# A two-layer diffusion backbone on one core: Pool's queue put in order by hand, modulation tiles requested one ahead, the last FFN product ended by output tile, and context squares moved

## The chip, the cores and the metric

The kernel runs on one core of one Trainium2 chip, as a single program. The metric is the device time of one execution in microseconds (us). The time before is a median of 1727.9 us over 3 runs (1726.85 to 1728.54).

A core has a matrix engine (TensorE, PE in the profile; PEld is its weight load), a vector engine (VectorE, DVE), an activation engine (ScalarE, ACT), GpSimd (POOL) and SyncE (SP). Here SP and POOL mainly issue DMA transfers; POOL's are those that add into their target, the saves of intermediate results, and most modulation tiles.

## The reference

Two transformer layers over 512 latent tokens with a context of 256 tokens, width 1024. Both token streams share the weights.

```python
for i in range(DEPTH):                      # DEPTH = 2
    mx = split(silu(c) @ ada_w[i] + ada_b[i], 6)        # shift, scale, gate; twice
    mc = split(silu(c_ctx) @ ada_w[i] + ada_b[i], 6)
    h_x = rms_norm(x, g1) * (1 + mx[1]) + mx[0]
    h_c = rms_norm(y_ctx, g1) * (1 + mc[1]) + mc[0]
    # layer 0: windowed attention with a sink; layer 1: retention in both directions
    out_c, out_x = mixer[i](h_x, h_c)
    x = x + mx[2] * out_x
    x = x + mx[5] * swiglu(rms_norm(x, g2) * (1 + mx[4]) + mx[3], ffn_w_in[i], ffn_w_out[i])
    if i == 0:                              # the context stream, likewise, with mc
        ...
return x
```

Layer 1 needs the context only as input of its keys and values. The modulation vectors of layer 1 (`mx`, `mc` of i = 1) are matrix-vector products of 1024 by 6144.

## The kernel before

Tokens lie along the free axis, features along the 128 partitions, so a [1024, 512] activation is eight tiles of 128 x 512. Each float32 operand is split into a high part (a cast to fp32r by ScalarE, `whi`) and a low part (the difference, by VectorE, `wlo`); a product is three matmuls: high by high, low by high, high by low (`split`, L169 and L170).

The stage that the diff touches is the FFN of layer 0 and the passage into layer 1. The FFN runs on latent and context tokens together (768 columns, two halves of 384, `THIRDS`), and both its products use a scheme of seven block products of half size.

**Loop over hidden tiles.** `pos` runs from 2 to 21. `seven(pos, jobs)` issues seven products of 12 matmuls; between them VectorE and ScalarE split the weights of this position and the next, and finish the activation of the position before (`last_gate`). After each odd position `pair_sums` (in the next position) forms sums and saves four tensors to device memory, four DMAs from POOL (L1063, L1065). `jobs[0]` follows the third product and `jobs[2]` the last: from position 5 both are `ada_next`, which computes one column of layer 1's modulation: a tile of 128 x 1024 weights is loaded by POOL into the tile `adaw` (one buffer) and VectorE multiplies it with the broadcast condition row and sums along it (L278), once or, for the tiles of both streams, twice.

At the ends of some positions stand steps that prepare weight sums for the second product in device memory: copies from SP and accumulating DMAs from POOL (`sum_add`, L824, 1280 KB each). Those within this loop stand at the ends of positions 3, 5, 7, 9, 11, 13 and 15; the accumulating ones are at 5, 7, 11 and 15.

**Second product.** For each of seven products (`prod`) there are 11 pairs of hidden tiles, two to a step (`m` from 0 to 5, the last step one pair). `fo_step` runs a step: for each pair, for each of four output tiles `d`, three matmuls. `fo_add` adds finished sums, scaled by the gate, to the streams: `xr` (latent) and `cres` (context). In the first five products every even step also does an `ada_next`; in the last product `late_sums` squares the new residual (`add_squares`), sums squares over the partitions by matmuls with a matrix of ones (`context_squares` for the context, `first_rms` for the first half of the latents), and normalises (`latent_norm`).

**Into layer 1.** `fo_add(o, 0, 1)` adds the last four output tiles. `values_first` runs the first product of the values (24 matmuls of 512 columns), then the last four context squares and their sums, the context norm (`context_norm`), the second half's row sum (`rms`) and its normalisation follow; then values, keys and queries.

**Order.** A planner lays out each engine's instructions from its own estimate of when each becomes ready. In the stretch `with tc.manual_schedule(engines=Hand)`, which covers the loop and the second product, the named engines take the program's order instead; instructions from outside the stretch may still be placed between. Before, `Hand` names PE, DVE, Activation and SP, so POOL's DMAs are the planner's. `after(ins, others)` adds an order without a semaphore. A buffer that is asked for again is waited for until its last reader is done, wherever the request stands in the program.

Of the kernel before, what the change touches and what calls it, by code (L numbers as in the profile page):

```python
# [11 lines left out]
AF = mybir.ActivationFunctionType  # L12
# [42 lines left out]
def dit_kernel(ctx, tc, xT, cT, crow, small, consts, masks, tabs0, tabs1, jtab, adaQ, adaN, adaT, wst, wgu, wfo, out):  # L55
# [37 lines left out]
    order = mybir.DependencyInfo(mybir.DependencyClass.NoSync, mybir.DependencyReason.DATA)  # L93
    turn = {"pre": None, "lnexp": [], "silu": []}

    def after(ins, others):
# [93 lines left out]
    def t_sq(n):  # L190
        return T(rp, 512, "sq", 2)[:, :n]
# [76 lines left out]
            silu(cr[:, i * 1024:(i + 1) * 1024], cr[:, i * 1024:(i + 1) * 1024])  # L268
        return cr

    def ada_tile(l, part, d, streams, cr, behind, room):

        j = part * 8 + d
        w, res = T(room, 1024, "adaw", 1 if l else 3), []
        (nc.gpsimd if l else nc.sync).dma_start(w, adaT[l, j])
        for s in streams:
            junk = T(rp, 1024, "y0", 1, BF16) if l else T(room, 1024, "junk", 1, BF16)
            res.append(nc.vector.tensor_tensor_reduce(junk, w, cr[:, s * 1024:(s + 1) * 1024], 1.0,  # L278
                                                      sm_t[:, C_ADAB + l * 48 + j:C_ADAB + l * 48 + j + 1], mult, add,
                                                      mods[l, s][:, part, d:d + 1]))  # L280
            after(res[-1], behind)
        return res
# [829 lines left out]

    def ada_next(behind=()):

        if ada_q:
            ada_tile(*ada_q.pop(0), cr, behind, fp)

    L_, R_ = slice(0, 512), slice(512, 1024)
    tile = {}
# [115 lines left out]
        split(fo[i][1], *w)  # L1235
        fo[i][1] = w

    def fo_step(i, o, first):
        x, w = fo.pop(i)
        n = x[0].shape[1] // 384  # L1240
        m = FO[i][1]
        for j in range(n):
            xs = [t[:, j * 384:(j + 1) * 384] for t in x]
            for d in range(4):
                ws = slice(j * 512 + d * P, j * 512 + (d + 1) * P)
                for e, (p, r) in enumerate(((w[0], xs[0]), (w[1], xs[0]), (w[0], xs[1]))):
                    nc.tensor.matmul(o[d], p[:, ws], r, start=first and 2 * m + j + e == 0,  # L1247
                                     stop=2 * m + j == PAIRS - 1 and e == 2, skip_group_check=True)

    def fo_add(o, d0, half, minus=False):  # L1250
        ends = []
# [22 lines left out]
    def context_squares(ds, first, last, behind=()):  # L1274
        for d in ds:
            sq = t_sq(SC)
            nc.scalar.activation(sq, cres[d], AF.Square)
            ins = nc.tensor.matmul(ctx_sum[0], ones, sq, start=d == first, stop=d == last, skip_group_check=True)
            after(ins, behind)
        return ins  # L1280

    def unit(u):
        w = [T(hq, 768, "aq", 20)[:, 0:512] for _ in range(KT - 4 * (u == 11))]
# [7 lines left out]
    ada_both = [(1, part, d, (0, 1)) for part in (0, 1) for d in range(KT)]  # L1291
    ada_one = [(1, part, d, (0,)) for part in (2, 3, 4, 5) for d in range(KT)]
    ada_q = [t for pair in zip(ada_both, ada_one) for t in pair] + ada_one[16:]
    wsel[0] = 0
    raws = [0]
    cr = None
# [60 lines left out]
    def nothing():  # L1357
        pass
# [16 lines left out]
    with tc.manual_schedule(engines=Hand):  # L1375
        for pos in range(2, FT):
            jobs = [nothing] * 3
            if pos == 2:
                jobs = [last_sum, gates_negated, nothing]
            elif pos == 3:  # L1380
                jobs[0] = rows_begin
            elif pos == 4:
                jobs[2] = rows_silu
            else:
# [12 lines left out]
        o = fo_y  # L1397
        for i, (prod, m) in enumerate(FO):
            if m == 0 and prod:
                o = fo_y if prod in (2, 4) else fo_z if prod == 5 else [bank("X"), bank("X"), pj(384), pj(384)] \  # L1400
                    if prod in (1, 3) else [bank("Y"), bank("Z"), bank("Z"), bank("Y")]
                if prod == 3:
                    fo_z = o
            if i == 0:
                fo_split_weights(1)
                last_gate(FT - 1)
            if i + 2 < len(FO):
                fo_split_weights(i + 2)
                fo_split_tokens(i + 2)
                fo_load(i + 3)  # L1410
            fo_step(i, o, prod in (0, 1, 3, 6))
            if m == (PAIRS - 1) // 2:
                for args in (((0, 0),), ((0, 0),), ((4, 0, True),), ((4, 1),), ((4, 1, True), (0, 1)), ((4, 0),), ())[prod]:
                    fo_add(o, *args)
            if prod < 5:
                ada_next() if m % 2 == 0 else None
            elif prod == 5:
                early_sums(m)
            else:
                late_sums(m)  # L1420
            if i == 2:
                Q.close()
                H = ExitStack()
                hpool[0] = H.enter_context(tc.tile_pool(name="hR", bufs=1, reuse_waits="tile", side="right"))
                h_rest += [(T(hpool[0], 512, "aq", 11, F32R), T(hpool[0], 512, "aq", 11, F32R)) for _ in range(4)]
                h_first += [T(hpool[0], 512, "aq", 11, F32R) for _ in range(3)]
                off_grid(hpool[0], 16)
                h_first.insert(0, T(hpool[0], 512, "aq0", 1, F32R))
                hm += [T(hpool[0], 512, "qk", 8) for _ in range(KT)]
    assert not ada_q  # L1430
    fo_add(o, 0, 1)
    F.close()
    E.close()

# [81 lines left out]
                                           stop=k == 3 and i == 2, skip_group_check=True)  # L1516
        return ins

    def product_v(os, a, w, first, tiles=(0, 1), by_k=False):

        for t, k in ((t, k) for k in range(4) for t in tiles) if by_k else ((t, k) for t in tiles for k in range(4)):
            tok = slice(t * P, t * P + P)
            whi, wlo = (p[:, k % 2 * 512:k % 2 * 512 + 512] for p in w[k // 2])
            xhi, xlo = (x[:, tok] for x in a(k))
            for i, (p, r) in enumerate(((xhi, whi), (xhi, wlo), (xlo, whi))):
                ins = nc.tensor.matmul(os[t], p, r, start=first and k + i == 0, stop=k == 3 and i == 2,  # L1526
                                       skip_group_check=by_k or not first)
        return ins
# [11 lines left out]
            res.append((hi, lo))  # L1540
        return res

    def strips(hd, behind=()):

        jt = T(qp, 1152, "rj", 1)
        nc.sync.dma_start(jt, jtab)
# [4 lines left out]
        lnexp(dx[:, 0:384], jt[:, 0:384], AF.Exp, scale=nlb, bias=dcol[:, 2, hd:hd + 1])  # L1551
# [4 lines left out]
        lnexp(dcx, jt[:, 0:640], AF.Exp, scale=lf, bias=dcol[:, 0, hd:hd + 1])  # L1556
        sums = []
        for c in (slice(0, 320), slice(320, 640)):
            e = t_hn(320) if hd else pj(320)
# [16 lines left out]
    def values_first(w, by_k=False):  # L1576

        Y = [W4("Z"), W4("Z")]
        ins = product_v(Y, quarter_of("11"), w, True, by_k=by_k)
# [3 lines left out]
        return w, Y, vt, ins  # L1583

    def context_values(w):
        c = [pj(), pj()]
# [2 lines left out]

    wsel[0] = 2  # L1590
    b11 = first_weights_v(0)
    b11, Yv, vt, ins = values_first(b11, True)
    context_squares(range(4), 4, 3, [ins])
    normed = context_norm([])
    add_squares(T1, range(4))
    rms(0, HALVES[1], behind=[ins])
    latent_norm(1, range(KT))
    for hd in range(RH):
        bq = chunk_base + 16 * hd
# [18 lines left out]
        k11, k21 = split_chunk(r11), split_chunk(r21)  # L1618
        if hd == 0:
            sums = token_sums(hm, 0, T(qp, 16, "sh2", 1), h_sum, [normed], (sub, add))  # L1620
            dx, dcx = strips(0, [sums])
        cos1, sin1 = rope_tables()
        Y, X, kc = W4("Y"), W4("X"), W4("X")
        kt, qt = [[T(qa, 512, "gate", 4) for _ in range(2)] for _ in range(2)]
# [212 lines left out]
            gated(t)  # L1837
        if not last:

            b11, Yv, vt, ins = values_first(first_weights_v(hd + 1))  # L1840
            transposes(1)
            transposes(0)
            turned(slice(0, SX))
# [365 lines left out]
```

## Time and profile before

| | us |
|---|---|
| median of 3 runs (lowest, highest) | 1727.9 (1726.85, 1728.54) |
| profiled execution | 1730.67 |
| its span, first to last instruction | 1728.7 |
| TensorE busy | 1685.8 |
| VectorE busy | 1340.9 |
| ScalarE busy | 893.1 |
| POOL busy | 116.6 |

The mean granted TensorE clock is 0.992 of full speed. In the profiled execution the loop over hidden tiles lies at 403 to 714 us from the span's start, the second product at 714 to 885, the first values of layer 1 behind that.

How to read the rows. An instruction in order of time has start, duration, engine, line, operation, output<-input, shape, and, in brackets, how long its engine stood idle before it and what ended that. A row of waits has total us, times, longest. A stretch of time has its length, then the busy time of PE, PEld, DVE, ACT and POOL with instruction counts, then the granted clock, the busy share of the DMA engines and GB/s. A DMA row ends with count, size of each and us from issue to landing; where there are several, that is the median. The "chain that ended last" lists pieces with start, duration and count.

### The profile page before, as it was taken

The page shows a single profiled execution, that of the slowest core. Times are in us where ns is not written, and L with a number is a line of the kernel's source. Part 1 is how long each engine was busy: PE and PEld are TensorE (multiplying, and loading weights), DVE is VectorE, ACT ScalarE, POOL GpSimd, SP SyncE. Part 2 cuts the span into 40 slices and gives each one's busy share as a digit, 9 for nine tenths or more (in the row PEclk, how much of TensorE's full clock was granted, in tenths as well). Part 3 has the DMA queues.
Part 4 walks back from the last instruction along what each step waited for, and adds up shares of the span by engine and source line. Part 5 has one row for each costly group of instructions (what it writes and reads, how often), then busy time and mean ns, then how long its engine had stood idle before and what let it go on. Part 6 is the DMA issues. An engine that isn't in the chain of part 4 may idle for free.

```text
span 1728.7 us, 27887 instructions
## 1 busy us (share of the span) xinstructions
PE 1685.8 (98%) x10798; PEld 1526.5 (88%) x10798; DVE 1340.9 (78%) x2395; ACT 893.1 (52%) x1565; POOL 116.6 (7%) x246
## 2 busy tenths in 40 slices
PE   8999999999989899999998999999999999999999
PEld 5878877899989899999978888888898899999997
DVE  6788888797678779778779857767757898876874
ACT  5678878474434334444555534534525565444442
POOL 0011111000111112100000000000000000000000
PEclk9999999999999999999999999999999999999999
DMA  9848967644867776898662634624624323333322
GB/s 383 303 93 195 238 141 190 219 153 159 253 194 240 246 219 213 302 307 286 196 160 61 187 107 103 184 69 124 193 64 110 122 74 106 114 109 110 100 86 85
DMA packets 113316, 293.87 MB, mean 170 GB/s; under 512 B 9520, under 2 KB 20288, under 8 KB 112928
## 3 DMA queue, kind: packets, MB, share of 16 engines
q1 hardware_dynamic: 87696, 218.75, 38.4%
q0 software_dynamic: 25200, 72.82, 17.8%
q8 instruction: 84, 1.38, 0.3%
q10 hardware_dynamic: 288, 0.52, 0.1%
q14 instruction: 48, 0.39, 0.1%
HBM read 274.82 MB, written 61.28 MB: 194 GB/s over the span
## 4 chain that ended last, share of the span: by engine, by line
PE 55%; DVE 6%; DMA 4%; issue 3%; ACT 1%; POOL 0%; POOLq 0%; DVEq 0%; ACTq 0%; SPq 0%
PE Y L965 8%; PE Z L1526 7%; PE Z L965 4%; PE Y L1515 3%; DMA adaw<-in_adaT_dram 3%; PE Y L1247 2%; PE Z L1247 2%; PE pj L152 2%; PE pj L154 2%; PE pj L153 2%; PE pj L1526 2%; PE pj L1247 2%; PE X L1247 2%; PE X L965 2%; PE X L1515 1%
## 5 line engine op out<-in xcount | busy, mean ns | idle before, releaser
L169 ACT CAST whi<-wraw 128x1024 fp32r<-128x1024 f32 (+1 forms) x285 | 295.3, 1040 | 323.3 <-PE Y L965 48.8
L170 DVE TENSOR_TENSOR wlo<-wraw,whi 128x1024 fp32r<-128x1024 f32 (+1 forms) x285 | 343.7, 1209 | 119.4 <-ACT whi L169 118.4
L965 PE MATMUL Y<-aq,whi 128*128 128x384 f32 x640 | 174.4, 338 | 0.0
L965 PE MATMUL Y<-aq,wlo 128*128 128x384 f32 x320 | 109.2, 341 | 13.3 <-DVE wlo L170 13.2
L965 PEld LDWEIGHTS Y<-aq,whi 128*128 128x128 f32 x640 | 118.4, 191 | 0.2
L278 DVE CUSTOM_DVE_ANT_0 y<-adaw,crow,small_sb 128x1024 bf16<-128x1024 f32 x64 | 82.1, 1282 | 43.5 <-DMA adaw<-in_adaT_dram 42.8
L1526 PE MATMUL Z<-whi,sA 128*128 128x512 f32 x256 | 80.6, 391 | 0.0
L106 ACT ACTIVATE pr<-pr,stat,qs 128x513 f32<-128x513 f32 (+2 forms) x96 | 74.1, 774 | 11.2 <-DVE stat L728 11.1
L965 PEld LDWEIGHTS Y<-aq,wlo 128*128 128x128 f32 x320 | 61.0, 191 | 15.7 <-DVE wlo L170 15.7
L152 PE MATMUL pj<-ax,whi 128*128 128x512 f32 x176 | 69.2, 393 | 0.5 <-DVE res L261 0.5
L154 PE MATMUL pj<-ax,whi 128*128 128x512 f32 x176 | 68.7, 390 | 0.0
L153 PE MATMUL pj<-ax,wlo 128*128 128x512 f32 x176 | 68.6, 390 | 0.0
L747 PE MATMUL pT<-const_sb,pr 128*128 128x128 f32 x352 | 56.6, 286 | 2.3 <-DVE pr L738 1.1
L261 DVE SCALAR_TENSOR_TENSOR res<-pj,mod,res 128x512 f32<-128x512 f32 (+1 forms) x64 | 45.3, 713 | 16.9 <-PE pj L154 16.8
L965 PE MATMUL Y<-sA,whi 128*128 128x256 f32 x304 | 58.1, 277 | 0.0
L722 DVE CUSTOM_DVE_ANT_0 pr<-S,mask,qs 128x256 f32<-128x256 f32 (+1 forms) x96 | 53.4, 567 | 5.6 <-PE S L721 4.4
L1526 PEld LDWEIGHTS Z<-whi,sA 128*128 128x128 f32 x256 | 48.0, 188 | 10.4
L965 PE MATMUL Y<-hx,whi 128*128 128x256 f32 x304 | 56.3, 277 | 0.0
L1247 PE MATMUL Y<-aq,whi 128*128 128x384 f32 x176 | 54.2, 343 | 0.0
L1247 PE MATMUL Z<-aq,whi 128*128 128x384 f32 x176 | 52.4, 338 | 0.0
L1526 PE MATMUL Z<-wlo,sA 128*128 128x512 f32 x128 | 50.5, 394 | 1.0 <-DVE wlo L170 1.0
L747 PEld LDWEIGHTS pT<-const_sb,pr 128*128 128x128 f32 x352 | 41.4, 145 | 11.2 <-issue 4.3
(591 smaller groups left out, 5102.4 us busy)
## 6 DMA issues: line engine op xcount, KB each, us to landing
wraw<-in_wst_dram SPq DMA_DIRECT2D x158, 512.0 KB, 3.7
adaw<-in_adaT_dram POOLq DMA_DIRECT2D x48, 512.0 KB, 4.0
op<-saved SPq DMA_DIRECT2D x35, 384.0 KB, 5.8
saved<-op POOLq DMA_DIRECT2D x33, 384.0 KB, 6.8
wraw<-in_wgu_dram SPq DMA_DIRECT2D x24, 512.0 KB, 4.7
gu_sum<-in_wgu_dram SPq DMA_DIRECT2D x8, 1280.0 KB, 13.2
gu_sum<-in_wgu_dram POOLq DMA_DIRECT2D x8, 1280.0 KB, 13.2
wraw<-fo_sum SPq DMA_DIRECT2D x20, 512.0 KB, 5.2
```

The costliest lines, as they stand in the source:

```text
L106: ins = nc.scalar.activation(*args, **kw)
L152: nc.tensor.matmul(o, whi, xhi, start=first, stop=False)
L153: nc.tensor.matmul(o, wlo, xhi, start=False, stop=False)
L154: return nc.tensor.matmul(o, whi, xlo, start=False, stop=last)
L169: after(nc.scalar.copy(hi, t), behind)
L170: return nc.vector.tensor_tensor(lo, t, hi, op=sub)
L278: res.append(nc.vector.tensor_tensor_reduce(junk, w, cr[:, s * 1024:(s + 1) * 1024], 1.0, sm_t[:, C_ADAB + l * 48 + j:C_ADAB + l * 48 + j ...
L747: nc.tensor.transpose(tp[:, a * P:(a + 1) * P], self.pr[(0, 2, 1, 3)[a]][:, ki * P:(ki + 1) * P], ident)
L965: nc.tensor.matmul(o, p, r, start=first and k + i == 0, stop=k == 3 and i == 2, skip_group_check=not first)
L1247: nc.tensor.matmul(o[d], p[:, ws], r, start=first and 2 * m + j + e == 0, stop=2 * m + j == PAIRS - 1 and e == 2, skip_group_check=True)
L1515: ins = nc.tensor.matmul(o[:, e * SC:(e + 1) * SC], p[:, ws], r, start=first and k + e + i == 0, stop=k == 3 and i == 2, skip_group_check= ...
L1526: ins = nc.tensor.matmul(os[t], p, r, start=first and k + i == 0, stop=k == 3 and i == 2, skip_group_check=by_k or not first)
```

## The change

Five edits. Modulation tiles are requested by a step of their own, `ada_ahead`, right behind the use of the tile before. POOL joins the engines ordered by hand, and within that stretch `after` adds no order. In the last product the steps `m` = 4 and 5 are joined, and the matmuls of the three pairs run output tile by output tile. Context squares 4 to 7 are formed two steps to one step sooner, and only their summing matmuls stay behind; the last additions `fo_add(o, 0, 1)` and the squares of what they make (`last_squares`) move into the hand-ordered stretch. The first values of layer 1 are cut in two, with the four context sums, the context norm and the row sum of the second half between the halves, TensorE's order there by hand.

```diff
     def after(ins, others):
-        for o in others:
+        for o in others if not by_hand[0] else ():
             tc.add_manual_dep(ins.ins, o.ins.name, order, reason="table set turn")
...
+    def ada_load(l, part, d, room):
+        w = T(room, 1024, "adaw", 1 if l else 3)
+        (nc.gpsimd if l else nc.sync).dma_start(w, adaT[l, part * 8 + d])
+        return w
...
     def ada_next(behind=()):
+        args = ada_q.pop(0)
+        ada_tile(*args, cr, behind, fp, ada_w.pop())
+        ada_ahead()
+
+    def ada_ahead():
         if ada_q:
-            ada_tile(*ada_q.pop(0), cr, behind, fp)
+            ada_w.append(ada_load(*ada_q[0][:3], fp))
...
-    def fo_step(i, o, first):
+    def fo_step(i, o, first, joined=False):
...            # parts_: the pairs of step i, and of i + 1 if joined
+        if joined:
             for d in range(4):
+                for part in parts_:
+                    one(*part, d)
+        else:
+            for part in parts_:
+                for d in range(4):
+                    one(*part, d)
...
+    def context_square(d, sq):
+        nc.scalar.activation(sq, cres[d], AF.Square)
+        ctx_sq[d] = sq
...            # context_total(ds, ...): the matmuls with ones over ctx_sq[d]
     def late_sums(step):
         if step < 2:
             add_squares(T0, (4 + 2 * step, 5 + 2 * step))
+            for d in (4 + 2 * step, 5 + 2 * step):
+                context_square(d, t_hn(SC))
         if step == 1:
             ctx_sum.append(pj(SC))
-        if step in (1, 2):
-            context_squares((2 * step + 2, 2 * step + 3), 4, 3)
-        if step == 1:
+            context_total((4, 5), 4, 3)
             first_rms()
+        if step == 2:
+            context_total((6, 7), 4, 3)
...
+    def last_squares():
+        y, c = ssq[0], slice(384, SX)
+        for d in range(4):
+            t = t_hn(512) if d < 2 else t_sq(512)
+            context_square(d, t[:, 0:SC])
+            sq = t[:, SC:SC + P]
+            nc.scalar.activation(sq, xr[d][:, c], AF.Square)
+            nc.vector.tensor_tensor(y[:, c], y[:, c], sq, op=add)
...
-    Hand = {mybir.EngineType.PE, mybir.EngineType.DVE, mybir.EngineType.Activation, mybir.EngineType.SP}
+    Hand = {mybir.EngineType.PE, mybir.EngineType.DVE, mybir.EngineType.Activation, mybir.EngineType.SP,
+            mybir.EngineType.Pool}
...            # position 4: ada_ahead() for the first tile
             for st in sum_turns.get(100 + pos, ()):
-                st(end)
+                st(None)
...
+            last = prod == 6 and m == (PAIRS - 3) // 2
+            if i + 1 < len(FO) or last:
+                fo_step(i, o, prod in (0, 1, 3, 6), last)
...
+        fo_add(o, 0, 1)
+        last_squares()
+        by_hand[0] = False
     assert not ada_q
-    fo_add(o, 0, 1)
...
-    b11, Yv, vt, ins = values_first(b11, True)
-    context_squares(range(4), 4, 3, [ins])
-    normed = context_norm([])
-    add_squares(T1, range(4))
-    rms(0, HALVES[1], behind=[ins])
+    ends = []
+
+    def totals():
+        context_total(range(4), 4, 3)
+        ends.append(context_norm([]))
+        ends.append(rms(0, HALVES[1]))
+
+    with tc.manual_schedule(engines={mybir.EngineType.PE}):
+        b11, Yv, vt = values_first(b11, totals)     # totals between k = 0, 1 and k = 2, 3
+    normed, other_rms = ends
     latent_norm(1, range(KT))
```

Two exponentials in `strips` are ordered behind the row sum of the second half (`soon=[other_rms]`).

More of the change, by code (lines that the diff above doesn't have):

```diff
@@ L1236, in fo_split_weights, with one @@
         fo[i][1] = w
-    def fo_step(i, o, first):
[L1239 to L1243, printed above, removed]
-            for d in range(4):
[L1245 to L1248, printed above, removed]
+    def fo_step(i, o, first, joined=False):
+        parts_, end = [], [fo.pop(j) for j in ((i, i + 1) if joined else (i,))]
+        k = 2 * FO[i][1]
+        for x, w in end:
+            n = x[0].shape[1] // 384
+            for j in range(n):
+                parts_.append((k, [t[:, j * 384:(j + 1) * 384] for t in x], w, j * 512))
+                k += 1
+        def one(k, xs, w, c, d):
+            ws = slice(c + d * P, c + (d + 1) * P)
+            for e, (p, r) in enumerate(((w[0], xs[0]), (w[1], xs[0]), (w[0], xs[1]))):
+                nc.tensor.matmul(o[d], p[:, ws], r, start=first and k + e == 0,
+                                 stop=k == PAIRS - 1 and e == 2, skip_group_check=True)
+        if joined:
+            for d in range(4):
+                for part in parts_:
[4 more added lines that the diff above has]
+                    one(*part, d)
     def fo_add(o, d0, half, minus=False):
@@ L1272, in add_squares, with context_total @@
                 nc.vector.tensor_tensor(ssq[0][:, cols], ssq[0][:, cols], sq, op=add)
-    def context_squares(ds, first, last, behind=()):
+    def context_square(d, sq):
+        nc.scalar.activation(sq, cres[d], AF.Square)
+        ctx_sq[d] = sq
+    def context_total(ds, first, last, behind=()):
         for d in ds:
-            sq = t_sq(SC)
-            nc.scalar.activation(sq, cres[d], AF.Square)
-            ins = nc.tensor.matmul(ctx_sum[0], ones, sq, start=d == first, stop=d == last, skip_group_check=True)
+            ins = nc.tensor.matmul(ctx_sum[0], ones, ctx_sq[d], start=d == first, stop=d == last, skip_group_check=True)
             after(ins, behind)
         return ins
+    ctx_sq = {}
     def unit(u):
@@ L1383, in dit_kernel @@
                 jobs[2] = rows_silu
+                ada_ahead()
             else:
@@ L1415, in dit_kernel @@
             if prod < 5:
-                ada_next() if m % 2 == 0 else None
+                ada_next() if m % 2 == 0 and ada_q else None
             elif prod == 5:
@@ L1517, in product_q, with product_v @@
         return ins
-    def product_v(os, a, w, first, tiles=(0, 1), by_k=False):
-        for t, k in ((t, k) for k in range(4) for t in tiles) if by_k else ((t, k) for t in tiles for k in range(4)):
+    def product_v(os, a, w, first, tiles=(0, 1), by_k=False, ks=range(4)):
+        for t, k in ((t, k) for k in ks for t in tiles) if by_k else ((t, k) for t in tiles for k in ks):
             tok = slice(t * P, t * P + P)
@@ L1541, in rope_pair, with strips @@
         return res
-    def strips(hd, behind=()):
+    def strips(hd, behind=(), soon=()):
         jt = T(qp, 1152, "rj", 1)
@@ L1582, in values_first @@
             nc.scalar.copy(vt[t], Y[t])
-        return w, Y, vt, ins
+        return w, Y, vt
     def context_values(w):
```

26 lines of the change are left out of this document (16 added, 10 removed).

## The prediction

> **What bounds the kernel now.** I read the page first, then who TensorE (PE) waited for, then TensorE's instructions in order of time, then Pool's and VectorE's (DVE's) around each hole, and last the landing times of single transfers.
>
> ```profile
> PE 1685.8 (98%) x10798; PEld 1526.5 (88%) x10798; DVE 1340.9 (78%) x2395; ACT 893.1 (52%) x1565; POOL 116.6 (7%) x246
> ```
>
> TensorE is the bound: of a span of 1728.7 us it is idle for 42.9. So no edit here can bring more than its holes and the slow clock behind them. Its waits in the stages that the diff touches:
>
> ```profile
> PE Y L965 <- DVE wlo L170: 13.2, 6, 5.7
> ...
> PE pj L1278 <- ACT sq L1277: 4.9, 2, 3.9
> ...
> PE Y L1515 <- ACT whi L169: 1.7, 1, 1.7
> PE Y L1515 <- DVE wlo L170: 1.6, 1, 1.6
> ```
>
> The first lies in the loop over hidden tiles, the second in the last product of the FFN, the third and fourth at the first keys of layer 1. The larger holes one by one, each in brackets at the end of its row:
>
> ```profile
> 482.83 0.44 PE L965 MATMUL Y<-aq,wlo 128*128 128x384 f32 x1 [1.33 <-DVE wlo L170]
> ...
> 511.98 0.69 PE L965 MATMUL Y<-aq,wlo 128*128 128x384 f32 x1 [3.92 <-DVE wlo L170]
> ...
> 578.12 0.69 PE L965 MATMUL Y<-aq,wlo 128*128 128x384 f32 x1 [5.73 <-DVE wlo L170]
> ...
> 870.46 2.07 PE L1278 MATMUL pj<-sq,ones_sb 128*128 128x256 f32 x4 [3.87 <-ACT sq L1277]
> ```
>
> A hole costs more than its length, because the granted clock (the third number from the end in these rows of stretches) is low after it:
>
> ```profile
> 510.00:515.00 5.00, 3.02 (x10) 3.02 (x11) 4.93 (x9) 1.05 (x2) 0.55 (x1) 0.66 0.44 124
> ...
> 576.00:580.00 4.00, 1.88 (x6) 1.88 (x7) 3.96 (x7) 0.00 (x0) 0.55 (x1) 0.53 0.38 88
> 580.00:584.00 4.00, 4.00 (x17) 4.00 (x16) 3.97 (x8) 2.86 (x4) 0.54 (x1) 0.61 0.36 111
> ...
> 872.00:874.00 2.00, 2.00 (x8) 1.91 (x7) 1.80 (x3) 0.58 (x2) 0.00 (x0) 0.50 0.01 2
> ```
>
> Lost behind the first: 0.34 x 5 = 1.7 us. Behind the second: 0.47 x 1.88 + 0.39 x 4 = 2.4. So some 2.1 each; the third, at half clock from 870.5 until about 876.5, 3.0. The loop loses 13.2 + 4.1 = 17.3 us in all.
>
> Why VectorE is late in the loop is on Pool. Four times there the same triple stands: an accumulating sum (L824), a saved pair (L1063), a modulation tile (L275).
>
> ```profile
> 455.78 1.20 POOL L824 DMA_DIRECT2D fo_sum<-in_wfo_dram  x1
> 461.08 0.76 POOL L1063 DMA_DIRECT2D saved<-op  x1 [4.09 <-DVE op L1051]
> 462.29 0.56 POOL L275 DMA_DIRECT2D adaw<-in_adaT_dram  x1 [0.45 <-DVE mod L278]
> ...
> 489.51 1.18 POOL L824 DMA_DIRECT2D fo_sum<-in_wfo_dram  x1
> 493.31 0.76 POOL L1063 DMA_DIRECT2D saved<-op  x1 [2.62 <-DVE op L1051]
> 494.52 0.55 POOL L275 DMA_DIRECT2D adaw<-in_adaT_dram  x1 [0.45 <-DVE mod L278]
> ...
> 554.41 1.18 POOL L824 DMA_DIRECT2D fo_sum<-in_wfo_dram  x1
> 557.95 0.76 POOL L1063 DMA_DIRECT2D saved<-op  x1 [2.36 <-DMA adaw<-in_adaT_dram]
> 559.44 0.55 POOL L275 DMA_DIRECT2D adaw<-in_adaT_dram  x1 [0.73 <-DVE mod L278]
> ...
> 618.23 1.18 POOL L824 DMA_DIRECT2D fo_sum<-in_wfo_dram  x1
> 623.57 0.76 POOL L1063 DMA_DIRECT2D saved<-op  x1 [4.17 <-DVE op L1051]
> 624.78 0.55 POOL L275 DMA_DIRECT2D adaw<-in_adaT_dram  x1 [0.45 <-DVE mod L278]
> ```
>
> Time from issue to landing (last number): all 48 tiles' median; the second sum; then the tiles of the four triples in order; last the final small save issued at 499.42:
>
> ```profile
> adaw<-in_adaT_dram POOLq DMA_DIRECT2D x48, 512.0 KB, 4.0
> ...
> fo_sum<-in_wfo_dram POOLq DMA_DIRECT2D x1, 1280.0 KB, 15.3
> ...
> adaw<-in_adaT_dram POOLq DMA_DIRECT2D x1, 512.0 KB, 10.9
> ...
> adaw<-in_adaT_dram POOLq DMA_DIRECT2D x1, 512.0 KB, 13.6
> ...
> adaw<-in_adaT_dram POOLq DMA_DIRECT2D x1, 512.0 KB, 14.8
> ...
> adaw<-in_adaT_dram POOLq DMA_DIRECT2D x1, 512.0 KB, 10.6
> ...
> saved<-op POOLq DMA_DIRECT2D x1, 192.0 KB, 11.6
> ```
>
> The sum issued at 489.51 lands at 504.8, the tile issued behind it at 508.1, the save at 511.0: on Pool's queue what is issued behind a sum lands behind it. From the sum's issue to the tile's landing it is 17.4, 18.6, 19.8 and 17.2 us; I call this L. VectorE then stands before its tile:
>
> ```profile
> 492.93 1.28 DVE L278 CUSTOM_DVE_ANT_0 y<-adaw,crow,small_sb 128x1024 bf16<-128x1024 f32 x1
> ...
> 494.45 1.22 DVE L170 TENSOR_TENSOR wlo<-wraw,whi 128x1024 fp32r<-128x1024 f32 x1 [0.23 <-ACT whi L169]
> ...
> 508.17 1.28 DVE L278 CUSTOM_DVE_ANT_0 y<-adaw,crow,small_sb 128x1024 bf16<-128x1024 f32 x1 [8.18 <-DMA adaw<-in_adaT_dram]
> ```
>
> Of those 8.18 us TensorE loses 3.92, since the weights split behind the middle tile of a position are wanted only by the next position's first product.
>
> **The change part by part.** *Tiles one ahead, Pool by hand.* There is one buffer for these tiles, so a request waits for VectorE to be done with the tile before; Pool already issued it 0.45 us after that. Requesting ahead by itself therefore brings nothing, and it adds no transfer. What moves is the sum: by hand it stands at the end of its position, behind the request that waits for that position's last tile. Near 490 it goes from 489.51 to 494.52 + 0.55 = 495.07; likewise to 462.85, 559.99 and 625.33. The tile that was late is now ahead of the sum (4.0 us is the median), so the 8.18 goes. Late next is the tile after it: it is requested when the next position's middle tile has been used (508.17 - 8.18 + 2 x 1.28 = 502.6), some 8 us after the sum, behind the sum and all four saves, and it belongs to the end of a position. On VectorE the split of the weights for the third product is queued behind that tile; TensorE has only two products in hand there, 12 matmuls each (first row; the second is for the values, below):
>
> ```profile
> 653.41 4.16 PE Y L965 x24
> ...
> 884.87 5.50 PE Z L1526 x24
> ```
>
> So the hole is: sum's issue + L + 2.6 (tile 1.28, split 1.22, and the step between) less the moment when TensorE wants the split. Near 490 that moment is 511.98 - 3.92 + 4.16 = 512.2, near 555 it is 578.12 - 5.73 + 4.16 = 576.6. The holes are L - 14.5 and L - 14.0. For L I take what the tiles needed before, plus 0.7: the same bytes are queued, but now all saves are ahead of the tile instead of one. The last save came 2.9 us behind the tile (511.0 against 508.1), which is the upper end. The lower end is a tile that lands 1.2 behind the sum's 15.3, L = 16.5. The 0.7 stays near the tile's own row, a quarter of the way up, since the saves have by then had the queue to themselves for longer than the tile. That gives 19.3 - 14.5 = 4.8 and 20.5 - 14.0 = 6.5; at the other two sums L is 1.9 shorter in the mean, and the moment is about 1 us later (482.83 - 1.33 = 481.5, less the small hole before it, 18 us after 462.85; 512.2 is 17 after 495.07), 2.5 each. Sum 16.3, against 13.2. With 2.1 of clock behind three of the four: 22.6 against 17.3, **+5.3 us**. Ends: L = 16.5 gives holes of 2.0, 2.5 and twice 1.0, no clock, 6.5, so -10.8; 2.9 instead of 0.7 makes every hole 2.2 longer and slows all four, 25.1 + 8.4 = 33.5, so +16.2.
>
> [...]
>
> *Context squares sooner.* The two holes, 1.0 and 3.9 of the 4.9 above, go with their slow clock: the squares now stand ahead of the row-sum chain on ScalarE (ACT). The second pair waits for its two buffers until TensorE has summed the first pair, which it does right after the product, 1.4 us of matmul by the row at 870.46 less its slow clock. Gain 1.0 + 3.9 + 3.0 = 7.9. The matmuls themselves stay.
>
> *Last product by output tile.* Same matmuls, but the single last pair is wanted six matmuls into the joined step instead of after 24. Its split ends late:
>
> ```profile
> 875.50 0.55 DVE L170 TENSOR_TENSOR aq<-op,aq 128x384 fp32r<-128x384 f32 x1
> ...
> 884.40 0.48 DVE L1328 SCALAR_TENSOR_TENSOR aq<-qk,mod,aq 128x256 fp32r<-128x256 f32 x1
> ...
> 893.89 0.43 DVE L204 SCALAR_TENSOR_TENSOR sq<-pj,sq 128x256 f32<-128x256 f32 x1 [6.25 <-ACT sq L203]
> ```
>
> It ended at 876.05 and comes about 1.9 sooner, as the squares leave the way: 874.1. TensorE ended the second step at 870.46 - 3.87 = 866.6; less the first hole of 1.0, plus sums of 1.4 and a step of 4.16, the joined step begins at 871.1 and wants the pair six matmuls (1.0) later. A hole of 2.0, between 0 and 4.
>
> The queue of loads on SP was by hand before and keeps its order; Pool's saves and its one memset stay behind the same VectorE work.
>
> *Sums amid the first values.* TensorE runs half of the first values (12 matmuls, half of the 5.50 us above), then by its own order the four sums, which need the last additions. These stand on VectorE behind the normalised tiles that ended at 884.88; I take 1.9 off for the squares and 1.1 for additions that ran amid them, 881.9, and an estimated 3.5 for eight additions and the last squares, in the proportion of the 0.48 of the row at 884.40: 885.4. TensorE is ready at 874.1 + 30 x 0.173 + 2.75 = 882.0, so it stands 3.4 us, between 0 and 5. In return the chain behind the sums starts some 6 us sooner: the 6.25 us in which VectorE stood before 893.89 are used. Who waits for the sums is the context norm and, behind it on VectorE, the key weights. The first keys then find their weights split: of the 3.3 us in two holes I take 3.0; with the clock there it could be 6. The two exponentials that now stand behind the second row sum are wanted by the scores, much later; ScalarE's 52% covers them, and they are costed at nothing. *Tail:* 7.9 - 2.0 - 3.4 + 3.0 = 5.5, so **-5.5 us** (ends 0 and -11).
>
> Sum +5.3 - 5.5 = -0.2. The profiled execution took 1730.67 us (span 1728.7), 2.8 over the median of the runs, 1727.9; I put the difference on the median: **1727.7 us**, no change that can be told. Within 0.2%, 3.5 us, I call it the same; a measurement of this kernel tells no less.
>
> **The rivals.** *A, faster:* the queue drains sooner behind the moved sum, L = 16.5. -10.8 - 5.5: 1711.6 us. For it: the first sum and the last were followed by tiles with L of only 17.4 and 17.2. Against: no tile had less. [...] *B, slower, where the forecast is no change:* the tile at the end of the position is truly last in Pool's queue and lands with the last save; L 2.9 longer. +16.2 - 5.5: 1738.6 us. For it: the save issued 9.9 us after the sum landed 21.5 after it, and the new request falls 8 us after it. Against: most of the saves' bytes were already queued around the late tile, and it still came before the last of them. It decides from an L of about 19.6 in the mean. *C, the tail gives nothing:* if the normalised tiles still end at 884.88, the sums wait 5 us and the clock falls again, 7.9 - 2.0 - 7.1 + 1.2 = 0. Then +5.3: 1733.2 us. For it: ScalarE and VectorE hand those tiles to and fro, which no edit shortens.
>
> **How the numbers follow.** Forecast 0.40, with a range of its own from 1720 to 1735; A 0.22; B 0.20; C 0.18. Faster by over 0.2% (below 1724.4): A and 0.12 of the forecast, 0.34. Slower (above 1731.4): B, 0.09 of the forecast and 0.12 of C, 0.41. The same: 0.25. The range runs from A to just past B, 1710 to 1739.
>
> **What would show it.** Right: each sum on Pool directly behind a tile request; the waits for tiles at the end of even positions instead of the middle; loop holes on the third product, about 16 us together; no wait on context squares; VectorE's stop before the context norm short. Wrong: loop holes under 7 us (A) or over 24 (B), a hole over 4 us before the row sums of the first values (C).

## The result, and the profile after

The changed kernel takes 1736.8 us (median of 5 runs, 1735.3 to 1738.88) against 1727.9 (1726.85 to 1729.91): ratio 1.0051, 95% interval 1.0036 to 1.0065. It is slower, by 8.9 us between the medians. The two profiled executions are only 4.6 us apart (1735.32, span 1733.2, against 1730.67): that of before was above all its timed runs, that of after near its lowest.

TensorE's waits in the changed kernel (in all, times, longest), the rows that answer to those of before:

```profile
PE Y L971 <- DVE wlo L172: 19.9, 4, 5.4
...
PE Y L1561 <- DVE wlo L172: 1.2, 2, 0.9
```

The loop's 13.2 us in six waits have become 19.9 in four; the waits for context squares are gone, and of the 3.3 us at the first keys 1.2 are left. The four loop holes in TensorE's timeline, each in brackets:

```profile
485.12 0.69 PE L971 MATMUL Y<-aq,wlo 128*128 128x384 f32 x1 [5.35 <-DVE wlo L172]
...
521.68 0.69 PE L971 MATMUL Y<-aq,wlo 128*128 128x384 f32 x1 [4.90 <-DVE wlo L172]
...
588.15 0.69 PE L971 MATMUL Y<-aq,wlo 128*128 128x384 f32 x1 [5.25 <-DVE wlo L172]
...
653.00 0.44 PE L971 MATMUL Y<-aq,wlo 128*128 128x384 f32 x1 [4.37 <-DVE wlo L172]
```

They are of nearly one size now, and the clock is low behind all four (stretches behind the first and the last; the granted clock is the third number from the end):

```profile
485.00:490.00 5.00, 4.88 (x15) 4.88 (x16) 3.69 (x7) 0.96 (x3) 0.00 (x0) 0.50 0.90 291
...
653.00:658.00 5.00, 5.00 (x20) 5.00 (x21) 3.90 (x6) 1.75 (x3) 0.00 (x0) 0.66 0.82 285
```

The missing clock times TensorE's busy time is 2.4 and 1.7 us, and 2.2 and 2.1 behind the two between (clock 0.50 and 0.56). Behind the second the next stretch, 526 to 531, still has 0.84, another 0.8. So the slow clock adds 9.2 us. Pool around the second sum:

```profile
498.49 0.53 POOL L275 DMA_DIRECT2D adaw<-in_adaT_dram  x1 [6.35 <-DVE mod L284]
499.01 1.18 POOL L830 DMA_DIRECT2D fo_sum<-in_wfo_dram  x1
499.70 1.23 POOL L1069 DMA_DIRECT2D saved<-op  x1
...
503.24 0.72 POOL L1069 DMA_DIRECT2D saved<-op  x1 [0.91 <-DVE op L1067]
503.95 0.58 POOL L1071 DMA_DIRECT2D saved<-op  x1
507.37 0.56 POOL L275 DMA_DIRECT2D adaw<-in_adaT_dram  x1 [2.84 <-DVE mod L284]
```

How long the sum, the first save, the two last saves (issued at 503.24 and 503.95) and the tile issued at 507.37 took from issue to landing (last number):

```profile
fo_sum<-in_wfo_dram POOLq DMA_DIRECT2D x1, 1280.0 KB, 15.0
...
saved<-op POOLq DMA_DIRECT2D x1, 384.0 KB, 15.7
...
saved<-op POOLq DMA_DIRECT2D x1, 384.0 KB, 14.3
saved<-op POOLq DMA_DIRECT2D x1, 192.0 KB, 14.0
...
adaw<-in_adaT_dram POOLq DMA_DIRECT2D x1, 512.0 KB, 11.8
```

Counted from the sum's issue, the sum lands at 15.0, the first save at 16.4, the two last at 18.5 and 18.9, and the tile, requested last, at 20.2. VectorE stands before it, and splits the third product's weights behind it:

```profile
519.20 1.28 DVE L284 CUSTOM_DVE_ANT_0 y<-adaw,crow,small_sb 128x1024 bf16<-128x1024 f32 x1 [7.52 <-DMA adaw<-in_adaT_dram]
```

In the four places L, the time from the sum's issue to the tile's landing, is 20.7, 20.2, 20.5 and 19.7 us. TensorE wants the split 17.8 us after the sum's issue each time (521.68 - 4.90 - 499.01), so a hole is L + 2.6 - 17.8: 5.5, 5.0, 5.3 and 4.5 against 5.35, 4.90, 5.25 and 4.37 in the rows.

The passage into layer 1, TensorE's rows and then VectorE's:

```profile
883.37 0.44 PE L1261 MATMUL Y<-aq,whi 128*128 128x384 f32 x1 [2.00 <-ACT aq L171]
...
893.90 1.35 PE L1303 MATMUL pj<-hn,ones_sb 128*128 128x256 f32 x4 [1.87 <-ACT hn L1298]
...
897.04 0.70 PE L227 MATMUL pj<-y,ones_sb 128*128 128x256 f32 x2 [0.49 <-DVE y L1394]
```

```profile
899.21 0.76 DVE L206 SCALAR_TENSOR_TENSOR sq<-pj,sq 128x256 f32<-128x256 f32 x2 [2.22 <-ACT sq L205]
```

The joined step has a hole of 2.00, the sums amid the first values 1.87 + 0.49 = 2.4, and VectorE's stop before the context norm is 2.22 instead of 6.25 us.

### The profile page after: what moved, and what is told of

It is laid out like the page before. It is cut to its first block, busy times and chain, and to the rows that moved or that the text cites. A ratio compares the mean times of both kernels' runs of the same rounds, so it can differ in the third digit from the quotient of the medians.

```text
span 1733.2 us, 27880 instructions
## 1 busy us (share of the span) xinstructions
PE 1685.6 (97%) x10798; PEld 1527.1 (88%) x10798; DVE 1343.0 (77%) x2395; ACT 895.0 (52%) x1565; POOL 116.2 (7%) x246
## 4 chain that ended last, share of the span: by engine, by line
PE 79%; DVE 8%; DMA 7%; ACT 3%; issue 2%; POOL 0%; SPq 0%; DVEq 0%; ACTq 0%
PE Y L971 13%; PE Z L1572 7%; PE Z L971 7%; PE pj L154 4%; PE pj L156 4%; PE pj L155 4%; PE X L971 3%; PE Y L1561 3%; DMA adaw<-in_adaT_dram 3%; PE S L727 2%; PE pT L753 2%; PE pO L775 2%; DVE wlo L172 2%; PE Z L1261 2%; PE Y L1261 2%; PE pj L1261 2%
## 5 line engine op out<-in xcount | busy, mean ns | idle before, releaser
L971 PE MATMUL Y<-aq,wlo 128*128 128x384 f32 x320 | 110.1, 344 | 19.9 <-DVE wlo L172 19.9
```

The lines of the kernel that those rows point to most:

```text
L971: nc.tensor.matmul(o, p, r, start=first and k + i == 0, stop=k == 3 and i == 2, skip_group_check=not first)
```

## The experiments

Medians are compared with runs of the kernel before on the same chip (1727.0 to 1729.9 in the four groups of runs). "Excess" is the time from start to start of TensorE's matmuls above 0.173 us for each 128x384 (4.16 / 24), summed from 440 to 720 us: holes and slow clock together. It is 19.3 before, 29.5 after.

**The two halves.** e1 keeps the tail's edits and takes the loop back; e2 does the loop alone.

```diff
# e1, from the changed kernel
-    Hand = {PE, DVE, Activation, SP, Pool}
+    Hand = {PE, DVE, Activation, SP}
...
-        args = ada_q.pop(0)
-        ada_tile(*args, cr, behind, fp, ada_w.pop())
-        ada_ahead()
+        if ada_q:
+            ada_tile(*ada_q.pop(0), cr, behind, fp)
...            # also: no ada_ahead() at position 4, `after` orders again, st(end)
# e2, from the kernel before: the reverse
```

> The loop as before (Pool by the planner, a tile requested where it is used), all edits of the last product and of the first values kept. Queue theory (the loop alone lost, the tail alone won): loop holes as before, 13 us in pieces of 3.9 and 5.7 at the first product of a position, tail as in the changed kernel; about 5.4 us under the kernel before, 1719 to 1725. Rival (the tail edits cost time that the one profile does not show): 1727 or more.

> Only the requests one ahead and Pool by hand; last product and first values as before. Queue theory: four holes of 4.4 to 5.4 us at the third product with a slow clock behind each, 9 to 14 us over the kernel before, 1737 to 1742. Rival (the loss is in the tail): 1726 to 1730.

e1: 1723.67 us, ratio 0.9968 [0.9956, 0.9979]. e2: 1741.89, ratio 1.0068 [1.0054, 1.0082]. The tail gains 5.3 us, the loop loses 12.9. Excess in the loop 19.3 and 29.1: e1's loop is that of before, e2's that of the change. The tail's step of the prediction held, the loop's did not.

**Are the sums the cause, and what carries them?** e3 leaves the four loop sums out. e4 keeps all their bytes, but cuts each into five pieces of 256 KB, each behind a tile request of its own; they are spread over positions 5 to 9, 11 to 15 and 17 to 21, and one copy on SP moves from the end of position 13 to that of 15.

```diff
# e3
-            for st in sum_turns.get(100 + pos, ()):
+            for st in sum_turns.get(100 + pos, ()) if pos not in (5, 7, 11, 15) else ():
# e4
-    spread(fo_steps(1), (103, 103, 105, 107, 109, 111, 113, 115))
...
+    one = lambda d, q, k: lambda: sum_add(t[d, k:k + 1], wfo[q, r0 + k:r0 + k + 1], None)
...
+    # two pieces to a position from 5, then one to a position: behind the middle
+    # request, the second behind that at the end
```

> The changed kernel with the four accumulating sums of the loop left out (positions 5, 7, 11, 15), so the second batch of weight sums is incomplete. Queue theory: the tiles behind them land about 4 us after issue, no hole over 1 us in the loop; 19.9 us of holes and some 10 of slow clock go, 1705 to 1711. Rival (Pool's fixed order itself holds the tiles, or the saves do): holes stay, over 1725.

> The changed kernel with each of the four sums cut into five of 256 KB, twenty in all, each behind a tile request (positions 5 to 9 two each, 11 to 15 and 17 to 21 one in the middle). The bytes are the same. Queue theory: a piece holds the queue some 3 us and the next request comes 7 us later, so holes vanish as without sums, 1706 to 1714. Rival (the DMA engines are short of bandwidth, wherever the bytes stand): tiles late again, many small holes, over 1722.

e3: 1702.96 us, 0.9848 [0.9833, 0.9863], excess 0.2. e4: 1706.06, 0.9861 [0.9846, 0.9877], excess 0.8. Without the sums no loop hole is left, and nearly the whole of that is to be had with the sums kept. The pieces' time from issue to landing in e4 (median of 20), and VectorE's stops for tiles between 440 and 720 us (in all, times, longest):

```profile
fo_sum<-in_wfo_dram POOLq DMA_DIRECT2D x20, 256.0 KB, 6.5
```

```profile
DVE y L284 <- DMA adaw<-in_adaT_dram: 23.9, 18, 4.0
```

A piece still takes 6.5 us, but a tile behind it is late by so little that VectorE's stops, 4.0 us at most, no longer reach TensorE. e4 beats both kernels: 1.4% under before, some 30 us under after. Cutting the sums and spreading them changed together; which of the two matters more no run shows.

**Is it the order of requests?** e6 moves nothing but the four saves in the position behind each sum, from ahead of the next tile request to behind it. e5 moves each sum to behind the middle request of its position.

```diff
# e6
+        if late_saves[0]:
+            late_saves.append(store)        # store: the four saves
...
     def ada_ahead():
             ada_w.append(ada_load(*ada_q[0][:3], fp))
+        while len(late_saves) > 1:
+            late_saves.pop()()
# e5
-                jobs[0] = jobs[2] = ada_next
+                jobs[0] = middle            # ada_next(), then the position's sum
+                jobs[2] = ada_next
```

> The changed kernel, but in the four positions with a sum the four saves are issued behind the next tile request instead of ahead of it. Theory (Pool's transfers are served in the order of their requests, so the tile at the end of the position is late for sum and saves together): the tile lands some 17 us after the sum's issue instead of 20, the holes shrink from about 5 to about 2 us each, 1722 to 1729. Rival (the same bytes are in flight around the tile either way, as my prediction argued): the landing stays at about 20 us, the holes near 5, 1734 to 1739.

> The changed kernel with its four loop sums issued behind the tile request in the middle of their position instead of the one at its end. Theory (the tile requested next after a whole sum is late, whichever it is; in the middle TensorE has more in hand than at the end): the late tile is again one that the next position's first product wants, the holes move from the third product to the first, and come to about the 13 us of before: 1721 to 1728. Rival (asking one ahead is itself what costs, by whatever place): the holes stay near 20 us, 1734 to 1739.

e6: 1714.21 us, 0.9912 [0.9893, 0.9931]. Pool's rows at its second sum, then how long the tile issued at 501.95 and the last save, issued at 504.66, took to land:

```profile
493.58 1.18 POOL L830 DMA_DIRECT2D fo_sum<-in_wfo_dram  x1
501.95 0.55 POOL L275 DMA_DIRECT2D adaw<-in_adaT_dram  x1 [7.19 <-DVE mod L284]
502.49 2.17 POOL L1071 DMA_DIRECT2D saved<-op  x3
504.66 0.57 POOL L1073 DMA_DIRECT2D saved<-op  x1
```

```profile
adaw<-in_adaT_dram POOLq DMA_DIRECT2D x1, 512.0 KB, 8.7
...
saved<-op POOLq DMA_DIRECT2D x1, 192.0 KB, 9.3
```

The request falls 8.4 us after the sum as in the changed kernel, yet the tile lands 17.1 us after the sum's issue (16.6 to 17.5 in the four places) and the saves only then, the last at 20.4. The order of requests decides, not the bytes in flight; this run refutes the ground on which I gave L only 0.7. e6 came out lower than its 1722 to 1729, since the holes shrank by 3.2 us in the mean (19.9 to 7.0 in all) and much of the slow clock went with them (excess 11.4).

e5: 1711.32 us, 0.9903 [0.988, 0.9927], again under its 1721 to 1728. The holes did move to the first product as the theory has it, but to 7.8 us, not 13: I had overlooked that the tile request behind the sum was now ahead of all four saves. Its tiles land 15.6 to 17.9 us after the sum.

**The loop's two edits apart.** e9 has the tiles one ahead, but leaves Pool to the planner; e10 has Pool by hand, but each tile requested where it is used. Both have the tail's edits.

> The changed kernel with its tiles still requested one ahead, but Pool's order left to the planner and the sums held back to the end of their position as before. Theory of my prediction (with one buffer, asking ahead by itself moves nothing): as the tail alone, 1721 to 1726. Rival (asking ahead is what puts the sum behind the later request, and so costs the loop its 13 us whoever orders Pool): 1734 to 1740.

> The changed kernel with Pool's order by hand, but each tile requested where it is used, not one ahead. The sum then stands behind the same request as before, and the late tile is again the middle one, but all four saves are ahead of it instead of one. Theory (served strictly in the order of requests): the tile lands about 20 us after the sum's issue instead of the 18 of before, each of the four holes is some 2 us longer, 1728 to 1734. Rival (only the place of the sum counts): as the tail alone, 1721 to 1726.

e9: 1716.1 us, 0.993 [0.9915, 0.9945]. e10: 1762.17, 1.0193 [1.017, 1.0216]. Each counted from the kernel before on its own chip, e1 stands at -5.3 us, e9 at -12.0, e10 at +34.1 and the change at +8.9. So against e1 asking ahead brings some 7 us, the order by hand costs some 39, and both together, the change, cost some 14: the two edits do not add up. None of my expectations allowed for that. Pool in e9, and the landing of its tile issued at 491.02:

```profile
486.01 1.18 POOL L830 DMA_DIRECT2D fo_sum<-in_wfo_dram  x1
491.02 0.55 POOL L275 DMA_DIRECT2D adaw<-in_adaT_dram  x1 [3.83 <-DVE mod L284]
491.55 0.74 POOL L1069 DMA_DIRECT2D saved<-op  x1
```

```profile
adaw<-in_adaT_dram POOLq DMA_DIRECT2D x1, 512.0 KB, 12.0
```

The request comes 5.0 us after the sum, as before (494.52 against 489.51), but no save is ahead of it: before, one was, issued 1.2 us earlier. L is 17.0 instead of 18.6 (15.8 to 17.0 in the four places). Pool has the same order as in e5 at all four sums, and the two profiled executions have nearly the same excess, 13.6 here and 13.9 in e5; that their medians lie 5 us apart stays open. The loop's wait row, and a stretch behind a hole of 2.24 us that ended at 506.85:

```profile
PE Y L971 <- DVE wlo L172: 11.0, 8, 2.2
```

```profile
507.00:512.00 5.00, 4.32 (x24) 4.00 (x24) 4.97 (x9) 2.86 (x4) 0.25 (x1) 1.00 0.56 161
```

Eight small holes instead of six (13.3 us in e1), and the clock stayed full behind all of them (0.998 in the mean of the span, 0.995 in e1): excess 13.6 against 19.3. In e10 the opposite: at its second sum Pool's rows are

```profile
501.85 0.71 POOL L1069 DMA_DIRECT2D saved<-op  x1 [0.92 <-DVE op L1067]
502.56 0.58 POOL L1071 DMA_DIRECT2D saved<-op  x1
503.12 0.57 POOL L275 DMA_DIRECT2D adaw<-in_adaT_dram  x1
...
534.31 0.72 POOL L1069 DMA_DIRECT2D saved<-op  x1 [4.07 <-DVE op L1057]
...
540.36 0.57 POOL L1071 DMA_DIRECT2D saved<-op  x1
540.92 0.56 POOL L275 DMA_DIRECT2D adaw<-in_adaT_dram  x1
```

The request stands behind four saves, the first three of which wait for VectorE (4.07 us in the row at 534.31). Beside a sum (503.12) it goes out 10.4 us after the sum and its tile lands after 21.4; in a pair without a sum (540.92) it is held as well. L is 20.9 to 22.1, and the loop's waits are

```profile
PE Y L971 <- DVE wlo L172: 38.2, 10, 7.1
```

**Is it the accumulating?** e7 makes the four sums plain copies of the same bytes.

```diff
+        how = {} if plain_sum[0] else {"accum_op": add}
-        after(nc.gpsimd.dma_start(flat(dst), flat(src), accum_op=add, max_dma_last_dim=ROW), ...)
+        after(nc.gpsimd.dma_start(flat(dst), flat(src), **how, max_dma_last_dim=ROW), ...)
```

> The changed kernel with the four loop sums turned into plain copies of the same bytes between the same places (the addition of the second operand is left out). Theory (it is the accumulating that takes 15 us): a copy lands in 7 to 10 us, by the 9.7 and 7.1 us that copies of 1280 KB took on SP's queue, the tile 8 us behind it is hardly late, the holes go, 1703 to 1709. Rival (it is the bytes and their two ends in DRAM): the copy takes 13 us or more, the holes stay near 5 us each, 1730 to 1738.

1712.65 us, 0.9901 [0.9884, 0.9919]: between the two expectations. The landing of the copies (median of the four):

```profile
fo_sum<-in_wfo_dram POOLq DMA_DIRECT2D x4, 1280.0 KB, 8.6
```

So 8.6 us instead of 13.7 to 15.6 (the sums of the changed kernel): the accumulating costs some 6 us of the sum. But the tile behind the saves still lands after 15.1 to 16.9 us, only 4 sooner, and in the profiled execution 3.9 us of waits at the loop's products are left. The theory was half right: the saves ahead of the tile are worth some 3 us of L by e6, the accumulating some 4.

**The tail's parts**, on e4, where the loop is quiet. e8 takes the joined step back, e11 puts the last row sums behind the whole of the first values, e12 does both, so that of the tail only the earlier squares stay.

```diff
# e8
-            if i + 1 < len(FO) or last:
-                fo_step(i, o, prod in (0, 1, 3, 6), last)
+            fo_step(i, o, prod in (0, 1, 3, 6))
# e11
-            product_v(Y, quarter_of("11"), w, True, by_k=True, ks=(0, 1))
-            between()
-            product_v(Y, quarter_of("11"), w, True, by_k=True, ks=(2, 3))
+            product_v(Y, quarter_of("11"), w, True, by_k=True)
+            between()
```

> The kernel with the sums in five pieces, but the last product of the FFN step by step as before, not its last two steps joined by output tile. Theory of my prediction (the joined step has a cost, its hole of 2.0 us, and what it gains at the end is covered): without it 1703 to 1705, about 2 us under the pieces' 1706.1. Rival (the joined step frees the first output tiles early, and the additions behind them are on the path): without it the hole goes, but the additions end 2 us or more later and TensorE stands before the row sums instead, 1706 to 1709.

> The kernel with the sums in five pieces, but the last row sums behind the whole of the first values instead of amid them. Theory of my prediction (the hole amid the values, 3.4 us by its sum and 2.4 measured, is about paid back by the 3.0 us won at the first keys): within 1.5 us of the pieces' 1706.1. Rival 1 (the move is all loss): 1703 to 1704.5, the hole gone and none at the first keys. Rival 2 (the move is what keeps the first keys fed): 1708 to 1711.

> The kernel with the sums in five pieces, with neither the joined step nor the row sums amid the first values; of the tail's edits only the earlier context squares are left. Theory (the two others come to nothing each, so the squares alone won the tail's 5.3 us): within 1.5 us of 1706.1. Rival (each of the two makes up for the other's absence, and together they carry part of the 5.3 us): 1708 to 1711.

e8: 1705.54 us; e11: 1706.27; e12: 1707.17; all against e4's 1706.06, whose runs spread from 1703.8 to 1707.0. Counted from the kernel before on their own chips, e8 lies 0.3 us under e4 by the ratios, e11 1.9 and e12 3.3 over it, and the intervals overlap. Neither part by itself is worth anything that shows. Waits of e4, of e8 and of e11 (L1276 is the joined step, L1318 the sums amid the values, L1584 the first keys):

```profile
PE Y L1276 <- ACT aq L171: 2.0, 1, 2.0
PE pj L1318 <- ACT hn L1313: 1.9, 1, 1.9
PE Y L1584 <- DVE wlo L172: 1.2, 2, 0.9
```

```profile
PE pj L1318 <- ACT hn L1313: 4.5, 1, 4.5
```

```profile
PE Y L1584 <- DVE wlo L172: 2.5, 2, 1.6
...
PE Y L1584 <- ACT whi L171: 1.1, 1, 1.1
```

Without the joined step its 2.0 us go and the sums' hole is 2.6 longer, so my prediction, which booked that step as a cost alone, missed what it gives; the theory of e8's expectation is not borne out. With the sums behind the values their hole goes, and the first keys wait 3.6 us instead of 1.2. Each part moves a hole. What remains of the tail's 5.3 us, 2 to 5 us, is the earlier squares, by difference; they were not run alone on the kernel before.

## Why the prediction was wrong

The forecast was 1727.7 us, no change; it came to 1736.8.

*Right.* Pool's order came out row for row: sum directly behind a tile request, four saves, then the late tile, 8 us after the sum. The holes moved to the third product. The clock costs 2.3 us a hole, for 2.1. The tail: -5.5 forecast, -5.3 in e1; the joined hole 2.0 as forecast, the sums amid the values 2.4 for 3.4, what they win at the first keys 2.4 for 3.0 (e11). Within it the squares were put at 7.9 and brought 2 to 5, while the two other parts, put at a loss of 2.4 together, came to something between nothing and a gain of 3.

*Wrong: the size of L.* I took before's L plus 0.7: 18.1, 19.3, 20.5 and 17.9, a mean of 19.0. Measured: 20.7, 20.2, 20.5 and 19.7, a mean of 20.3, and 20.2 in e2. In the mean L grew by 2.0, not 0.7. My ground for 0.7, that the saves' bytes were queued around the late tile in any case, fell in e6: a tile behind the saves lands behind them, a tile ahead of them 3 us sooner. In before one save was ahead of the tile. I also carried before's L over place by place. In e1, whose loop is that of before, the same places have 16.5, 19.5, 17.1 and 19.0, so L differs from one execution to the next and only the means compare. That is why 2.5 us of hole were forecast at the first and last sum, and 5.35 and 4.37 came. At the other two 4.8 and 6.5 were forecast, and 4.90 and 5.25 came. There a second error helped: TensorE wanted the split 17.8 us after the sum, where I had 17.1 and 16.6. With all four holes long, all four were slowed, where I slowed three. Holes of 19.9 instead of 16.3 and 9.2 instead of 6.3 for the clock make the loop after 6.5 us dearer than forecast.

*Rival B.* Its mechanism held: the tile is last in Pool's queue and lands behind the last save, and L is above the 19.6 from which B decides. Its price did not. It added 2.9 to L where 2.0 came, its sign (over 24 us of holes) was not met, and its loop at +16.2 is too dear beside e2's +12.9. So its 1738.6, near the 1736.8, is in part luck.

*The base.* I put the loop at 17.3 us lost before and 22.6 after. By excess, less the 0.2 that e3 keeps without any sum, it lost 19.1 and 29.3. Before's waits and its two slow stretches I had read rightly; most of the 1.8 us that I was short of is what a count from start to start adds at each of the six holes, 0.2 to 0.3 us. That is +10.2 between the profiled executions, and with the tail's -5.3 it gives 4.9, close to their difference of 4.6. The other 2.7 us up to e2's +12.9 lie between profiled and timed executions, as before's profiled execution lay above its timed ones. Which holes vary from run to run stays open: the timed runs show none.

*Wrong: "Requesting ahead by itself therefore brings nothing".* It brings some 7 us (e9), because it takes a save from ahead of the tile: L falls from 18.0 to 16.4 in the mean (e1 to e9), the holes by 2.3 us, and the slow clock behind the two long ones goes. And the order by hand was costed as a move of the sum; by itself it costs some 39 us (e10), because on a queue in program order a request also waits for what the saves ahead of it wait for. I added the two edits as one step and so saw neither.

## What to carry to other kernels

On a queue that lands transfers in the order of their requests, cost a late transfer by the bytes ahead of it, not by those around it, and list for each moved request what now stands ahead of it and what those wait for. Small transfers with a consumer near the bound go ahead of large ones without one; a large one is cut into pieces small enough to hide (five of 256 KB, spread out, brought 30 us here, with every byte kept). When two edits touch one queue, cost each alone and then the pair: here one gained some 7 us, the other lost some 39, and together they lost some 14.

## What the runs showed of the hardware

In the loop of the changed kernel an accumulating transfer between two places in device memory took 13.7 to 15.6 us for 1280 KB. The plain copy in the same places took 8.6 (e7), and an accumulating piece of 256 KB 6.5 (e4).

In the profile of before all 128 of Pool's transfers landed in the order of their requests, and so did the 128 of the changed kernel; in the rows above the last saves land at 18.5 and 18.9 us and the tile at 20.2.

A low clock does not need a long hole. In e6 TensorE stood idle for 1.64 us of 508 to 513 and for 0.16 behind that, 1.80 in all, and the stretch from 513 has a granted clock of 0.66; it stood idle for 1.60 us of 570 to 575, and the clock behind that is full:

```profile
508.00:513.00 5.00, 3.36 (x20) 3.04 (x18) 2.33 (x3) 1.92 (x4) 0.56 (x1) 1.00 0.77 307
513.00:518.00 5.00, 4.84 (x19) 4.84 (x20) 3.70 (x7) 1.83 (x3) 0.00 (x0) 0.66 0.89 280
570.00:575.00 5.00, 3.40 (x20) 3.08 (x19) 2.64 (x4) 1.81 (x4) 0.56 (x1) 1.00 0.74 297
575.00:580.00 5.00, 5.00 (x30) 5.00 (x31) 4.06 (x6) 2.71 (x5) 0.00 (x0) 1.00 0.95 310
```

All four holes of the changed kernel, 4.4 to 5.4 us, have a low clock behind them as well, 0.50 to 0.66 in the stretches above. What a hole costs is read from the measured stretch.

The length of a hole is not the whole of it, for in e9 the clock stayed full behind one of 2.24 us. The traces of before and of the changed kernel show how the two go together there. In both the low clock, but for that at the very end of the span, stands in stretches of 3.41 or 6.83 us that begin on one grid of 3.41 us (in the loop of the changed kernel at 483.18, 520.73, 585.58 and 653.85). I counted TensorE's idle time in every interval at full clock between 260 and 1690 us of the two profiles. Each of the 8 with 2.57 us or more was followed by the low clock, and none of the others, which have 1.80 or less. So in these two profiles the low clock goes with the idle time within one interval. A sharp bound is not shown: 1.80 us was not enough there, and in e6 the low clock came behind as much. No run was made to test this.
